# A hybrid decoder layer: where and when the kept gate/up results are loaded

## The chip, the cores and the metric

The kernel runs on one core of one Trainium2 chip. The metric is the device time of one execution in microseconds; the median of 3 runs of the kernel before the change is 1995.07 us (1994.6 to 1999.07).

## The reference, cut to what matters

One decoder layer in fp32: a mixing sub-layer (windowed attention and a convolution group side by side, one output projection) and a dense SwiGLU feed-forward, each between two RMS norms. There are 2048 tokens of width 1024, and the feed-forward's inner width is 2816. The change lies in the feed-forward:

```python
h = rms_norm(x, ffn_pre_g)
h = (silu(h @ w_gate) * (h @ w_up)) @ w_down
x = x + rms_norm(h, ffn_post_g)
```

## The kernel before

**Arithmetic.** Every fp32 operand is split into a rounded high part (ScalarE, line 824) and the rest (a subtraction on VectorE, line 828, which the trace books under line 94, the helper that records all of VectorE's operations). A product is then high·high + high·low + low·high: for a block of 128 output rows, 512 inner and 512 tokens that is 4 × 3 = 12 matmuls (line 85), called a *product* below.

**Tiling.** Tokens go in tiles of 512, and the feed-forward takes two tiles at a time: the first pair (names with @F and @G up to some 1340 us) and the second pair. Each 2 × 2 block product of weights by tokens is done with seven products instead of eight (a Strassen-Winograd scheme): sums of weight blocks (S1 to S4, line 1005, tile `chl`) meet sums of token blocks (T1 to T4). `MATS` lists 22 matrices, gate and up by turns, one for each of 11 blocks of inner rows.

**The stages of a pair.** `stage_pre` (line 916) computes for the first 20 matrices (16 in the second pair) the two products that need only the plain token blocks, and stores their sum to DRAM in `keeps`. `stage_p1` (line 986) then goes through the 22 matrices: five products where a result was kept, seven where not. For a matrix with a kept result:

- `fetch` (lines 1028 to 1032) loads the kept tile into the ring `gb` (two buffers) by SP's queue; it is called in the fourth of the five products of the matrix before (line 1100).
- at the matrix's first product ScalarE copies the kept tile into PSUM bank B (line 1060). This copy is called the *seed*. The first product goes to bank C, the second to bank B, on top of the seed.
- the first product's result y5 is taken out of PSUM by ScalarE into the ring `gb` (line 1071), the second's, x2, into the ring `at` (two buffers, line 1074). VectorE adds later products to them (line 1078), ScalarE applies silu (line 1081), VectorE multiplies gate by up, and the results go to DRAM in `mids` (lines 1088 to 1097).
- weight blocks for the matrix after next are loaded at the last product (lines 1000, 1002).

Beside the first pair's `stage_p1` runs `stage_tsums` (line 1106): for each of the 11 blocks it loads four blocks of w_down (line 1113, ring `wx` of one tile for two of them, ring `fc` of three for the others), waits, makes four subtractions on VectorE (names wx@G and fc@G) and stores each to DRAM (`td`, line 1119). Its `yield` numbers are amounts of work of the main stage: it is pumped at a rate of 0.3.

After `stage_p1` comes `stage_p2` (line 1144), the down projection: its first two token operands use the ring `at` (lines 1162, 1163), the following ones `fa`.

**What sets the order.** Generators are interleaved by their yields, and a tile scheduler turns that into one fixed order of instructions for each engine and each queue. SP's queue issues nearly all transfers, one after the other; an issue that waits for a buffer holds those behind it.

Of the kernel before, what the change touches and what calls it, by code (L numbers as in the profile page):

```python
# [37 lines left out]
def layer_kernel(ctx, tc, x, xT, cols, rows, sinks, relb, onehot, w_in, w_pw, w_out, w_gate, w_up, w_down, out):  # L38
    nc = tc.nc
# [15 lines left out]
    def t_(tag, shape, dt=F32):  # L55
        return sb.tile(list(shape), dt, tag=tag, name=nm(tag), bufs=BUFS[tag])

    def f4(tag, shape=(P, D)):
        return t_(tag, shape)

    def f2(tag, shape=(P, T)):
        return t_(tag, shape)

    def hl(tag):
        return t_(tag, (P, 2, T), F32R)
# [757 lines left out]
    def split_f(x, w):  # L823
        act(w[:, 0], x, AF.Copy)  # L824
        return w

    def lo(x, w, on_pool):
        (ptt if on_pool else vtt)(w[:, 1], x, w[:, 0].bitcast(F32), ALU.subtract)
# [79 lines left out]
    def product(o, w, op, first):  # L908
        n = 0
        for k in range(4):  # L910
            ks = slice(k * P, (k + 1) * P)
            for a, b in ((0, 0), (0, 1), (1, 0)):
                mat(o, w[:, a, ks], op[k][:, b], start=first and n == 0, stop=n == 11, skip_group_check=not first)
                n += 1
# [71 lines left out]
    def stage_p1(ws, ops, mid, keep):  # L986
        PRE = PRES[ws[0]]
        L = f"F{ws[0]}"
        raws = {}
        todo = []  # L990
        for m in range(len(MATS)):
            st = [1, 2, 4, 5, 6] if m < PRE else list(range(7))
            todo += [(m, j, i, len(st)) for j, i in enumerate(st)]

        def loads(m):
            if m < len(MATS):
                lab[0] = L
                src, pr = MATS[m]
                r0 = t_("raw", (P, 2, T))
                nc.sync.dma_start(r0, src[2 * pr].rearrange("p (a b) -> p a b", a=2))  # L1000
                r1 = t_("chl", (P, 2, T))
                nc.sync.dma_start(r1, src[2 * pr + 1].rearrange("p (a b) -> p a b", a=2))
                raws[m] = dict(A11=r0[:, 0], A12=r0[:, 1], A21=r1[:, 0], A22=r1[:, 1])

        def sums(m):
            if m < len(MATS):
                lab[0] = L
                r = raws[m]
                s12 = t_("chl", (P, 2, T))
                r["S1"], r["S2"] = s12[:, 0], s12[:, 1]  # L1010
                vtt(r["S1"], r["A21"], r["A22"], ALU.add)
                vtt(r["S2"], r["S1"], r["A11"], ALU.subtract)
                s34 = t_("chl", (P, 2, T))
                r["S3"], r["S4"] = s34[:, 0], s34[:, 1]
                vtt(r["S3"], r["A11"], r["A21"], ALU.subtract)
                vtt(r["S4"], r["A12"], r["S2"], ALU.subtract)

        wops = {}
        kept = {}

        def split(q):
            if q < len(todo):
                m, j, i, n = todo[q]
                lab[0] = L
                wops[q] = split_f(raws[m][STEPS[i][1]], hl("w"))
                lo(raws[m][STEPS[i][1]], wops[q], ws[0] and i in POOL_LO)

        def fetch(m):
            if m < PRE:
                lab[0] = L  # L1030
                kept[m] = f2("gb")
                nc.sync.dma_start(kept[m], keep[m])

        loads(0)
        sums(0)
        for q in range(AHEAD):
            split(q)
        loads(1)
        fetch(0)
        sg = {}  # L1040
        for q, (m, j, i, nst) in enumerate(todo):
            pre = m < PRE
            gate = MATS[m][0] is w_gate
            pr = MATS[m][1]
            split(q + AHEAD)
            lab[0] = L
            which, an, bn = STEPS[i]
            if len(ops.get(bn, ())) < 4:
                lh.until(f"S{ws[0]}")
                lab[0] = L  # L1050
            if j == 0:
                bk = {}
                if not gate:
                    blocks = {}
                    if pre:
                        blocks[3] = f2("fa")
                        nc.sync.dma_start(blocks[3], mid[0, pr])
                if pre:
                    bk["B"] = mm()
                    act(bk["B"], kept.pop(m), AF.Copy)  # L1060
            first = which not in bk
            if first:
                bk[which] = mm()
            o = bk[which]
            product(o, wops.pop(q), ops[bn], first)
            if i == 0:
                bk["B"] = mm()
                act(bk["B"], o, AF.Copy)
            elif i == 1:
                y5 = f2("gb")  # L1070
                act(y5, o, AF.Copy)
            elif i == 2:
                x2 = f2("at")
                act(x2, o, AF.Copy)  # L1074
            else:
                v = {4: y5, 5: x2}.get(i, o)
                if v is not o:
                    vtt(v, v, o, ALU.add)
                if gate:
                    s = f2("fa")  # L1080
                    act(s, v, AF.Silu)
                    sg[i] = s
                else:
                    s = sg.pop(i)
                    vtt(s, s, v, ALU.mult)
                    blocks[i] = s
                    if i in (3, 4, 6):
                        nc.sync.dma_start(mid[{3: 0, 4: 4, 6: 1}[i], pr], s)
                    if i == 5:
                        a11, a22, a21 = blocks[3], blocks[4], s  # L1090
                        for to, o_, p_, op, q_ in ((5, a22, a21, ALU.add, a22), (3, a21, a11, ALU.subtract, a21),
                                                   (2, a11, a22, ALU.subtract, a11)):
                            (ptt if ws[0] else vtt)(o_, p_, q_, op)
                            nc.sync.dma_start(mid[to, pr], o_)
                    if i == 6:
                        (ptt if ws[0] else vtt)(s, s, blocks[3], ALU.subtract)
                        nc.sync.dma_start(mid[6, pr], s)
            if j == nst - 4:
                sums(m + 1)
            if j == nst - 2:  # L1100
                fetch(m + 1)
            if j == nst - 1:
                loads(m + 2)
            yield 2.76

    def stage_tsums(td):
        L = "G0"
        for pr in range(NF // 2):
            lab[0] = L
            wx = f4("wx", (P, 2, T))  # L1110
            b = [wx[:, 0], wx[:, 1], f2("fc"), f2("fc")]
            for i, (f, n) in enumerate(((0, 0), (0, 1), (1, 0), (1, 1))):
                nc.sync.dma_start(b[i], w_down[2 * pr + f, :, n * T : (n + 1) * T])
            yield 3
            b11, b12, b21, b22 = b
            for to, o, p_, q_ in ((0, b11, b12, b11), (2, b12, b22, b12), (1, b22, b22, b11), (3, b21, b21, b22)):
                lab[0] = L
                vtt(o, p_, q_, ALU.subtract)
                nc.sync.dma_start(td[to, pr], o)
                yield 1  # L1120

    def finish(L, gb, jobs, pool=True):
        lab[0] = L
# [317 lines left out]
    ws, ops = (0, 1), {}  # L1441
# [5 lines left out]
    lh.add("S0", stage_h_sums(ws, ops), lambda: f"P0.{PRE_S0}" in started and "B3" in lb.done)  # L1447
    run(stage_pre(ws, ops, mids[0], keeps[0], Q0))
    lt.add("TS", stage_tsums(td))
    run(stage_p1(ws, ops, mids[0], keeps[0]))  # L1450
    lt.until("TS")
    lc.until("T2")
    lc.rates["T3"] = RC3
    ws, ops = (2, 3), {}
# [9 lines left out]
    run(stage_pre(ws, ops, mids[1], keeps[1]))  # L1464
    lf.until("E0.3")
    run(stage_p1(ws, ops, mids[1], keeps[1]))
    run(stage_p2(ws, mids[1], td, True))

# [62 lines left out]
```

## Time and profile before

| | |
|---|---|
| median of 3 runs | 1995.07 us |
| the profiled execution | 1997.41 us |
| its span, first to last instruction | 1995.4 us |
| mean granted TensorE clock | 0.990 |
| gate/up stage of the first pair | 675 to 987 us |
| down stage of the first pair | 987 to 1340 us |
| gate/up stage of the second pair | 1449 to 1782 us |

A view by windows gives for each stretch the busy time of PE (TensorE's matmuls), PEld (its weight loads), DVE (VectorE), ACT (ScalarE) and POOL (GpSimd), the granted clock and the DMA share. The views of waits list what an engine stood still for: the engine and instruction that waits, an arrow, what released it, and then the us in total, how often, and the longest. A timeline row gives start, duration, engine, line, operation, output<-input, and in square brackets the idle time just before with what ended it. SPq is SP's queue issuing a transfer.

### The profile page before, as it was taken

How to read it: one execution, taken by the hardware profiler on the slowest of the kernel's cores; microseconds unless marked ns; L12 is line 12 of the kernel's file. 1: busy time of each engine (PE TensorE's matmuls, PEld its weight loads, DVE VectorE, ACT ScalarE, POOL GpSimd, SP SyncE). 2: the span in 40 equal slices, each digit the busy share in tenths (PEclk: the TensorE clock that was granted, in tenths of full speed). 3: DMA queues.
4: the chain of work that ended last, by engine and by line, in shares of the span. 5: the costliest groups of instructions: out<-in, count | busy, mean ns of one | idle time of the engine just before them, and what ended most of it. 6: DMA issues, size and time to landing. Idle time of an engine off the chain costs nothing. (4 is left out here: it accounts for less than half of the span.)

```text
span 1995.4 us, 26645 instructions
## 1 busy us (share of the span) xinstructions
PE 1933.4 (97%) x8730; PEld 1547.1 (78%) x8730; DVE 1465.0 (73%) x2578; ACT 952.6 (48%) x1878; POOL 327.0 (16%) x415
## 2 busy tenths in 40 slices
PE   8999999999998999999999999996999999999997
PEld 6877777777777778778878788884788888888886
DVE  4999969995876898887669954576666665555557
ACT  4455354447547533334444555464534433345443
POOL 4011011101122100000000110044423332311003
PEclk9999999999999999999999999998999999999999
DMA  8786657566659868875478876779745542466664
GB/s 302 253 306 216 209 188 256 183 208 219 232 188 347 269 205 268 302 235 173 148 239 266 298 262 201 252 257 334 238 144 177 169 152 92 136 234 191 215 192 146
DMA packets 224811, 444.06 MB, mean 223 GB/s; under 512 B 22137, under 2 KB 47905, under 8 KB 224673
## 3 DMA queue, kind: packets, MB, share of 16 engines
q1 hardware_dynamic: 207584, 420.35, 63.7%
q10 hardware_dynamic: 17088, 22.02, 3.0%
q8 instruction: 68, 1.11, 0.2%
q14 instruction: 71, 0.57, 0.1%
HBM read 327.46 MB, written 114.83 MB: 222 GB/s over the span
## 5 line engine op out<-in xcount | busy, mean ns | idle before, releaser
L94 DVE SCALAR_TENSOR_TENSOR fc@C<-glu@C,colt,fc@C 128x512 f32<-128x512 f32 x480 | 356.5, 756 | 2.8
L85 PE MATMUL mm@F<-hl@H,w@F 128*128 128x512 f32 x1056 | 253.4, 390 | 5.6 <-ACT mm@F L953 4.6
L85 PEld LDWEIGHTS mm@F<-hl@H,w@F 128*128 128x128 f32 x1056 | 197.5, 188 | 48.5 <-ACT mm@F L953 6.3
L85 PE MATMUL mm@G<-hl@G,hl@G 128*128 128x512 f32 x924 | 227.7, 392 | 2.9 <-DVE hl@G L94 1.8
L85 PE MATMUL mm@A<-hl@A,w@A 128*128 128x512 f32 x840 | 209.5, 397 | 4.7 <-ACT w@A L127 2.3
L85 PEld LDWEIGHTS mm@G<-hl@G,hl@G 128*128 128x128 f32 x924 | 171.7, 188 | 39.6 <-DVE hl@G L94 2.5
L824 ACT ACTIVATE w@F<-chl@F 128x512 fp32r<-128x512 f32 x220 | 135.2, 625 | 136.4 <-PE mm@F L85 130.7
L85 PE MATMUL mm@G<-w@G,hl@G 128*128 128x512 f32 x876 | 199.4, 389 | 0.0
L85 PEld LDWEIGHTS mm@G<-w@G,hl@G 128*128 128x128 f32 x876 | 164.4, 188 | 34.1
L85 PEld LDWEIGHTS mm@A<-hl@A,w@A 128*128 128x128 f32 x840 | 156.6, 189 | 43.5 <-issue 3.1
L94 DVE TENSOR_TENSOR w@F<-chl@F,w@F 128x512 fp32r<-128x512 f32 x198 | 145.5, 739 | 37.5 <-ACT w@F L824 37.2
L85 PE MATMUL mm@F<-mid@H,w@F 128*128 128x512 f32 x528 | 138.8, 411 | 15.6 <-ACT mm@F L953 10.4
L85 PE MATMUL mm@F<-ql@H,w@F 128*128 128x512 f32 x528 | 130.7, 395 | 13.9 <-ACT mm@F L1060 5.3
L85 PEld LDWEIGHTS mm@F<-mid@H,w@F 128*128 128x128 f32 x528 | 104.6, 199 | 40.6 <-ACT mm@F L953 11.5
L85 PE MATMUL mm@F<-p@H,w@F 128*128 128x512 f32 x528 | 129.0, 389 | 0.0
L85 PEld LDWEIGHTS mm@F<-ql@H,w@F 128*128 128x128 f32 x528 | 99.7, 190 | 37.8 <-ACT mm@F L1060 6.5
L85 PE MATMUL mm@F<-x@H,w@F 128*128 128x512 f32 x528 | 126.8, 391 | 0.0
L85 PEld LDWEIGHTS mm@F<-p@H,w@F 128*128 128x128 f32 x528 | 99.0, 188 | 20.7 <-ACT at@F L1074 0.2
L85 PEld LDWEIGHTS mm@F<-x@H,w@F 128*128 128x128 f32 x528 | 98.4, 188 | 21.5 <-DVE fc@C L94 0.8
L495 POOL TENSOR_SCALAR_AFFINE_SELECT p@B<-p@B 128x512 f32<-128x512 f32 x62 | 52.3, 853 | 363.4 <-ACT p@B L493 362.0
L127 ACT ACTIVATE w@A<-raw@A 128x512 fp32r<-128x512 f32 x110 | 67.4, 625 | 93.0 <-PE mm@A L85 61.0
L94 DVE TENSOR_TENSOR w@G<-raw@G,w@G 128x512 fp32r<-128x512 f32 x73 | 52.2, 715 | 68.6 <-ACT w@G L824 67.7
(302 smaller groups left out, 3299.7 us busy)
## 6 DMA issues: line engine op xcount, KB each, us to landing
mids<-fa@F SPq DMA_DIRECT2D x154, 256.0 KB, 2.6
raw@A<-w_in SPq DMA_DIRECT2D x55, 512.0 KB, 4.5
w@A<-lo_in SPq DMA_DIRECT2D x84, 256.0 KB, 3.4
fc@G<-mids SPq DMA_DIRECT2D x77, 256.0 KB, 3.5
fa@G<-mids SPq DMA_DIRECT2D x75, 256.0 KB, 4.4
gb@F<-keeps SPq DMA_DIRECT2D x72, 256.0 KB, 4.1
w@W<-fold SPq DMA_DIRECT2D x32, 512.0 KB, 5.3
chl@F<-w_gate SPq DMA_DIRECT2D x22, 512.0 KB, 4.0
```

Source lines behind the costliest of these rows:

```text
L85: r = nc.tensor.matmul(*args, **kw)
L94: r = op(*args, **kw)
L127: act(w[:, 0], raw, AF.Copy)
L495: nc.gpsimd.affine_select(out=pg[:, kb].rearrange("p (i q) -> p i q", q=P), in_=pg[:, 1].rearrange("p (i q) -> p i q", q=P), compare_op=AL ...
L824: act(w[:, 0], x, AF.Copy)
```

## The change

There are four edits. The first pair's kept results are loaded by GpSimd's queue, the second pair's still by SP's. y5 goes to the ring `at` beside x2, so that the ring `gb` holds kept results alone within the stage. `fetch(m + 1)` is called in the second product of a matrix (j = 1). In `stage_tsums` 5 units instead of 3 lie between a block's loads and its first subtraction, and 0.5 instead of 1 after each subtraction: 7 in all as before.

```diff
@@ stage_p1, fetch
-                nc.sync.dma_start(kept[m], keep[m])
+                (nc.sync if ws[0] else nc.gpsimd).dma_start(kept[m], keep[m])
@@ stage_p1, first product of a matrix
-                y5 = f2("gb")
+                y5 = f2("at")
@@ stage_p1
-            if j == nst - 2:
+            if j == 1:
                 fetch(m + 1)
@@ stage_tsums
-            yield 3
+            yield 5
...
-                yield 1
+                yield 0.5
```

What SP's queue does around one kept load in the middle of the first pair's gate/up stage: weight loads and stores of the w_down sums (td) around it. Before:

```order
L1119 DMA td<-fc@G_1373_8310 128x512
L1113 DMA wx@G_1403_8516<-w_down 128x512 x2
L1119 DMA td<-fc@G_1372_8309 128x512
L1113 DMA fc@G_1404_8517<-w_down 128x512
L1088 DMA mids_4716<-fa@F_1310_7903 128x512
L1032 DMA gb@F_1351_8163<-keeps_4719 128x512
L1113 DMA fc@G_1405_8518<-w_down 128x512
L1119 DMA td<-wx@G_1403_8516 128x512
```

And the same place of SP's queue after the change:

```order
L1119 DMA td<-wx@G_1371_8308 128x512
L1119 DMA td<-fc@G_1373_8310 128x512
L1119 DMA td<-fc@G_1372_8309 128x512
L1113 DMA wx@G_1403_8516<-w_down 128x512 x2
L1088 DMA mids_4716<-fa@F_1311_7903 128x512
L1113 DMA fc@G_1404_8517<-w_down 128x512
L1113 DMA fc@G_1405_8518<-w_down 128x512
L1119 DMA td<-wx@G_1403_8516 128x512
```

The kept load (L1032) stands behind two stores and a store to mids before, and is gone from SP's queue after; the loads of the w_down blocks still follow the stores of the block before. On GpSimd the 20 loads stand in one piece with nothing between them, and each waits only for the seed that frees its buffer.

The second place is ScalarE at that seed, with the evictions of y5 (L1071) and x2 (L1074) and the high parts of weights (L824). Before:

```order
L1071 ACTIVATE gb@F_1339_8092<-mm@F_1338_8079 128x512
L824 ACTIVATE w@F_1340_8096<-chl@F_1320_7952 128x512
L824 ACTIVATE w@F_1347_8126<-chl@F_1342_8113 128x512
L1074 ACTIVATE at@F_1341_8111<-mm@F_1337_8077 128x512
L824 ACTIVATE w@F_1349_8145<-chl@F_1342_8113 128x512
L824 ACTIVATE w@F_1352_8165<-chl@F_1343_8116 128x512
L1060 ACTIVATE mm@F_1358_8192<-gb@F_1351_8163 128x512
L824 ACTIVATE w@F_1356_8187<-chl@F_1343_8116 128x512
```

After:

```order
L824 ACTIVATE w@F_1336_8072<-chl@F_1329_7997 128x512
L1060 ACTIVATE mm@F_1358_8192<-gb@F_1344_8119 128x512
L824 ACTIVATE w@F_1340_8096<-chl@F_1320_7952 128x512
L1071 ACTIVATE at@F_1339_8090<-mm@F_1338_8077 128x512
L824 ACTIVATE w@F_1348_8128<-chl@F_1342_8113 128x512
L1074 ACTIVATE at@F_1341_8111<-mm@F_1337_8075 128x512
```

The seed of the next matrix (mm@F_1358) has moved from behind the evictions of y5 and x2 to ahead of them.

The third place is VectorE where a block of w_down sums meets the addition to y5 (gb@F before, at@F_1252 after). Before:

```order
L94 TENSOR_TENSOR chl@F_1272_7645<-chl@F_1272_7645,raw@F_1264_7599 128x512
L94 TENSOR_TENSOR chl@F_1273_7648<-raw@F_1264_7599,chl@F_1272_7645 128x512
L94 TENSOR_TENSOR wx@G_1257_7529<-fc@G_1259_7531,wx@G_1257_7529 128x512
L94 TENSOR_TENSOR gb@F_1252_7503<-gb@F_1252_7503,mm@F_1250_7488 128x512
L94 TENSOR_TENSOR fc@G_1259_7531<-fc@G_1259_7531,wx@G_1257_7529 128x512
L94 TENSOR_TENSOR at@F_1254_7521<-at@F_1254_7521,mm@F_1251_7490 128x512
```

After:

```order
L94 TENSOR_TENSOR w@F_1263_7580<-chl@F_1256_7526,w@F_1263_7580 128x512
L94 TENSOR_TENSOR chl@F_1273_7644<-raw@F_1264_7599,chl@F_1272_7641 128x512
L94 TENSOR_TENSOR wx@G_1258_7531<-fc@G_1260_7533,wx@G_1258_7531 128x512
L94 TENSOR_TENSOR fc@G_1260_7533<-fc@G_1260_7533,wx@G_1258_7531 128x512
L94 TENSOR_TENSOR at@F_1252_7501<-at@F_1252_7501,mm@F_1250_7486 128x512
L94 TENSOR_TENSOR fc@G_1259_7532<-fc@G_1259_7532,fc@G_1260_7533 128x512
L94 TENSOR_TENSOR at@F_1254_7521<-at@F_1254_7521,mm@F_1251_7488 128x512
```

The sum that reads a w_down block (wx@G<-fc@G) stands ahead of y5's addition in both, with one more sum between them after the change.

At the end of the stage, TensorE's order has 36 matmuls of the second pair's out-projection (names tr@W) ahead of the first matmul of the down stage (mm@G), which before stood between the down stage's first ones.

## The prediction

> **What bounds the kernel now.** I read the page's busy line first, then the table by stage, then what TensorE waits for inside the one stage that the change touches most.
>
> ```profile
> PE 1933.4 (97%) x8730; PEld 1547.1 (78%) x8730; DVE 1465.0 (73%) x2578; ACT 952.6 (48%) x1878; POOL 327.0 (16%) x415
> 675.00:987.00 312.00, 299.16 (x1304) 244.38 (x1303) 261.67 (x419) 116.82 (x209) 0.00 (x0) 0.99 0.68 224
> 1449.00:1782.00 333.00, 333.00 (x1469) 275.40 (x1469) 200.13 (x261) 129.15 (x229) 97.14 (x68) 1.00 0.46 154
> ```
>
> TensorE is busy for 1933.4 of 1995.4 us, and the change neither adds nor removes a matmul. So it can only give back TensorE's idle time, or add some. The second and third lines are the gate/up stages of the first and the second pair (columns: window, its us, then busy us of PE, PEld, DVE, ACT, POOL, then the granted clock, DMA share, GB/s). The first pair has 312.00 − 299.16 = 12.8 us of idle PE; the second has none (333.00 of 333.00), so its sixteen kept loads, moved as well, can gain nothing. GpSimd computes nothing in the first pair (0.00).
>
> Next, the waits of PE from 675 to 987 us (us in total, times, longest), and under them the largest wait of ScalarE there:
>
> ```profile
> PE mm@F L85 <- ACT mm@F L1060: 5.3, 2, 4.2
> PE mm@F L85 <- ACT w@F L824: 3.0, 1, 3.0
> PE mm@F L85 <- DVE gb@F L94: 2.7, 3, 1.1
> PE mm@F L85 <- ACT gb@F L1071: 1.0, 1, 1.0
> PE mm@F L85 <- DVE fa@F L94: 0.9, 1, 0.9
> PE mm@F L85 <- ACT mm@F L953: 0.3, 1, 0.3
> ACT mm@F L1060 <- DMA gb@F<-keeps: 56.1, 16, 10.1
> ```
>
> The six PE rows add to 13.2, which is the idle time. L1060 is the seed: ScalarE copies the kept result into PSUM, and the matrix's product on bank B may start only then. ScalarE itself waits 56.1 us for the kept tiles, up to 10.1 at once. Most of that costs nothing; it costs where PE runs dry behind it.
>
> **The change, part by part.** *1. The kept loads come sooner.* The issue and landing of a kept load now:
>
> ```profile
> L1032 SPq DMA_DIRECT2D gb@F<-keeps x36: 319/402/698, 668.8 to 1633.1; - x36
> DMA to landing us min/median/max: 2.6/3.8/7.0
> 797.71 0.42 SPq L1032 DMA_DIRECT2D gb@F<-keeps  x1
> 803.07 0.60 ACT L1060 ACTIVATE mm@F<-gb@F 128x512 f32<-128x512 f32 x1 [10.05 <-DMA gb@F<-keeps]
> 803.61 0.61 ACT L824 ACTIVATE w@F<-chl@F 128x512 fp32r<-128x512 f32 x1
> 804.27 0.74 PE L85 MATMUL mm@F<-ql@H,w@F 128*128 128x512 f32 x2 [2.98 <-ACT w@F L824]
> 861.69 0.43 SPq L1032 DMA_DIRECT2D gb@F<-keeps  x1
> 866.44 0.60 ACT L1060 ACTIVATE mm@F<-gb@F 128x512 f32<-128x512 f32 x1 [8.31 <-DMA gb@F<-keeps]
> 867.09 1.07 PE L85 MATMUL mm@F<-ql@H,w@F 128*128 128x512 f32 x2 [4.19 <-ACT mm@F L1060]
> 867.96 2.76 PE L85 MATMUL mm@F<-mid@H,w@F 128*128 128x512 f32 x6
> 870.52 1.64 PE L85 MATMUL mm@F<-mb@H,w@F 128*128 128x512 f32 x6
> 872.00 2.44 PE L85 MATMUL mm@F<-ql@H,w@F 128*128 128x512 f32 x10
> 874.28 1.52 PE L85 MATMUL mm@F<-yt@H,w@F 128*128 128x512 f32 x6
> 875.64 1.52 PE L85 MATMUL mm@F<-mid@H,w@F 128*128 128x512 f32 x6
> ```
>
> At both places SP issues the load about 5 us before the seed, with a transfer of 3.8, so whatever delays SP lands on the seed. At 804 the 3.0 that the wait table books on L824 belongs here too: that split is queued behind a seed that held ScalarE for 10.05 us. At 867 PE waits 4.2 and is then slow: 24 matmuls from 867.09 to 874.28 take 7.19 us, where six at pace take 875.64 − 874.28 = 1.36, so 24 take 5.44. That is 1.75 more, which goes with the wait.
>
> The order shows the loads alone on GpSimd's queue, held only by the seed that frees their buffer (two matrices back). A matrix is five products of 2 × 1.36 = 2.72, so 13.6 us, and the lead becomes up to 27 us against 5. I take the two rows, 5.3 + 3.0, as gone, and 1.75 with them: **−10.05**. The 1.1 at 704, the smaller of the two L1060 waits, is not banked:
>
> ```profile
> 704.47 1.43 PE L85 MATMUL mm@F<-ql@H,w@F 128*128 128x512 f32 x5 [1.14 <-ACT mm@F L1060]
> 711.34 1.66 PE L85 MATMUL mm@F<-yt@H,w@F 128*128 128x512 f32 x6 [1.13 <-DVE gb@F L94]
> 700.00:760.00 60.00, 56.77 (x248) 46.04 (x247) 57.11 (x93) 23.52 (x42) 0.00 (x0) 1.00 0.64 211
> 795.00:825.00 30.00, 27.02 (x118) 21.99 (x119) 27.44 (x46) 10.50 (x19) 0.00 (x0) 1.00 0.85 288
> 825.00:860.00 35.00, 34.44 (x151) 27.77 (x150) 27.43 (x45) 12.37 (x22) 0.00 (x0) 1.00 0.88 295
> 860.00:890.00 30.00, 25.81 (x107) 20.84 (x106) 26.01 (x43) 9.22 (x17) 0.00 (x0) 0.94 0.70 226
> ```
>
> DVE is busy 57.11 of 60 us from 700 to 760, and PE waits for it 7 us later anyway: there what is late next is DVE, and I give the 1.1 back: **+1.1**. The large two lie where DVE has room: from 795 to 890 it idles 2.6 + 7.6 + 4.0 = 14.1 us, and the gain asks 8.95 of them.
>
> *2. The issue on GpSimd.* SP is spared 20 issues of 0.40. What writing one such load costs on GpSimd is in no row: this kernel has no load there yet. What GpSimd and DVE cost each other is shown only for computing, in the second pair:
>
> ```profile
> L94 DVE TENSOR_TENSOR w@F<-chl@F,w@F 128x512 fp32r<-128x512 f32 x106 | 72.0, 684 | 4.9 <-ACT w@F L824 4.8
> L94 DVE TENSOR_TENSOR w@F<-chl@F,w@F 128x512 fp32r<-128x512 f32 x83 | 67.4, 815 | 29.6 <-ACT w@F L824 29.3
> L1093 POOL TENSOR_TENSOR fa@F<-fa@F,fa@F x31: 1287/1298/1628, 1472.5 to 1780.9; 128x512 f32<-128x512 f32 x31
> L1060 ACT ACTIVATE mm@F<-gb@F x36: 590/602/604, 675.9 to 1636.9; 128x512 f32<-128x512 f32 x36
> ```
>
> The first row is DVE's split in the first pair, the second the same work beside GpSimd's 68 operations: 684 becomes 815 ns. Over its 200.13 us DVE loses at most about 200.13 × 131/815 = 32 us, 0.47 per GpSimd operation. Ends for the 20 loads: nothing, and 20 × 0.47 = 9.4 us of DVE, of which the stage can hide what DVE idles. The seeds start at 675.9 and come every 13.6 us, so seven fall before 760, where DVE idles least: 7 × 0.47 = 3.3. I take half of that, **+1.6**, nearer to nothing since a load computes nothing on GpSimd; the ends stay 0 and 9.4.
>
> *3. Longer lead for the w_down sums, and y5 in the x2 ring.*
>
> ```profile
> 793.51 0.69 DVE L94 TENSOR_TENSOR wx@G<-fc@G,wx@G 128x512 f32<-128x512 f32 x1 [1.30 <-DMA fc@G<-w_down]
> 794.12 0.68 DVE L94 TENSOR_TENSOR gb@F<-gb@F,mm@F 128x512 f32<-128x512 f32 x1
> 794.85 1.66 PE L85 MATMUL mm@F<-yt@H,w@F 128*128 128x512 f32 x6 [1.01 <-DVE gb@F L94]
> ```
>
> A sum that waits for its w_down block holds y5's addition behind it, and PE waits 1.0: this is the form of the 2.7 on DVE. The order moves the sums by one to four DVE operations only, at this place the waiting sum still stands ahead of y5's addition, and the w_down loads still follow the stores that free their ring. Gain between −1.0 (a new such wait) and 2.7; I take **−0.7**, near the one place where an operation of 0.69 is put in between.
>
> *4. Hand-over to the down stage.* In the first pair y5 now shares a ring with the down stage's first two operands:
>
> ```profile
> 995.07 0.38 SPq L1163 DMA_DIRECT2D at@G<-mids  x1
> 1008.78 0.68 DVE L94 TENSOR_TENSOR fa@F<-fa@F,gb@F 128x512 f32<-128x512 f32 x1
> 1018.48 2.79 PE L85 MATMUL mm@G<-hl@G,hl@G 128*128 128x512 f32 x11 [1.09 <-ACT hl@G L824]
> ```
>
> The operand load of 995.07 must now wait for y5's last reader (1008.78, about 1004 once no down matmul stands ahead of it). The order puts 36 matmuls of the out-projection (8.2 us at 1.36 per six) ahead of the first down matmul, more than load and split need (3.8 + two of 0.7). Ends: −1.1 (the wait of 1018) and +3; I take **+0.5**.
>
> **Sum.** −10.05 + 1.1 + 1.6 − 0.7 + 0.5 = −7.55. The profiled execution took 1997.41 (span 1995.4), so it would take 1989.9; it lies 2.34 over the median of 1995.07, and against the median the forecast is **1987.5**.
>
> **The rivals.** *A. DVE becomes the bound.* For it: 57.11 of 60 busy from 700, and 27.44 of 30 around the wait at 804. If the 3.0 there comes back as a wait for DVE, and GpSimd costs the 3.3 in full, the sum is −10.05 + 1.1 + 3.0 + 3.3 − 0.7 + 0.5 = −2.85: 1992.2. Against it: the 7.6 us that DVE idles right behind.
>
> *B. Slower: GpSimd gets to write its loads only when DVE pauses.* Place: 675 to 760, seven seeds, DVE at 57.11 of 60. A load delayed past its 27 us of lead costs landing plus seed, 3.8 + 0.6 = 4.4 us of PE. Four late seeds are 17.6; against the −7.55 the time is 1995.07 + 10.05 = 2005. It decides from two late seeds on (8.8 > 7.55). Against it: GpSimd's computing in the second pair ran at a median of 1298 ns with a shortest of 1287 and a longest of 1628, so DVE held it for 0.34 us at most. The Trainium skill, "SBUF — State Buffer", section "Who interferes with whom", has this mechanism as a trap: a load issued from GpSimd stands still while DVE is in a two-port mode, and elsewhere on that page 620 ns become about 3100. The same section says that tensor_tensor has no such mode and bars only GpSimd's reads; by the trap each load would land 2.5 us later, which is an estimate from that page and far inside the lead, so by it the sum stays. No run yet shows a load issued there.
>
> *C. It doesn't do what it says.* With five products a matrix the fetch moves from the fourth to the second, two products, and the w_down sums hardly move. If landing is slow because the DMA engines are full (share 0.85 and 0.88 from 795 to 860), the waits stay: 1995. Against it: 10.05 us of waiting for a transfer of 3.8, with the issue itself late.
>
> **How the numbers follow.** A measurement of this kernel tells about 0.3% from no change, 6 us: faster is below 1989.1, slower above 2001. The forecast has 0.60 (1981 to 1991, over its bounds: the low end is 1995.07 less 12.8 idle and 1.75 clock), A 0.18, C 0.07, B 0.15. Of the forecast's 0.60 some five sixths lie below 1989.1: faster 0.50; same is the rest of it with A, C and the mild end of B, 0.37; slower 0.13. The range runs from 1981 to 2000: B's upper part and the odd end are left out.
>
> **What would show it.** Right: the wait of L1060 for keeps near 0 in the first pair, the issues of L1032 there on GpSimd with 15 us or more to the seed; PE idle from 675 to 987 down from 12.8 to about 4; no slow matmuls at 867; DVE's split still near 684 ns. A: new PE waits for DVE (at@F or w@F) between 795 and 890, or that split above 700 ns. B: landing times on GpSimd's queue above 20 us and L1060 still waiting before 760. Wrong at the hand-over: PE idle over 3 us before the first down matmuls. The whole is wrong if the stage shortens by 9 us and the span doesn't.

## The result and the profile after

The changed kernel is slower: 2006.1 us median against 1998.59 before (10 runs each, the three shown above among them), ratio 1.0041 with a 95% interval of 1.0031 to 1.0050. On another chip, run again beside the rest, it was 1.0031 (1.0020 to 1.0041). The forecast was a gain of 0.4%. Part of the distance between 2006.1 and the forecast 1987.5 is the basis: it was reckoned from a median of 1995.07 over three runs, and over ten runs the kernel before stands at 1998.59. What is left is a gain of 7.55 us forecast and a loss of 7.5 measured. Executions of one kernel scatter by some 5 us to either side here, so a single profile settles nothing under that size; the ratios do.

The profile of after, its busy line and the stretches that the prediction used for before (the first pair's gate/up stage, and the hand-over behind it):

```profile
PE 1941.8 (97%) x8730; PEld 1551.4 (77%) x8730; DVE 1470.4 (73%) x2578; ACT 955.1 (48%) x1878; POOL 337.2 (17%) x435
675.00:987.00 312.00, 297.48 (x1272) 241.26 (x1271) 256.79 (x412) 114.14 (x202) 9.68 (x18) 0.98 0.68 225
990.00:1020.00 30.00, 30.00 (x134) 24.83 (x133) 15.99 (x27) 13.81 (x27) 0.00 (x0) 1.00 0.58 188
```

The same 312 us hold 1272 matmuls where they held 1304. At full pace (1.36 us per six) 32 matmuls are 7.3 us; the spans differ by 2002.2 − 1995.4 = 6.8. So the loss lies in this stage. PE idles 14.5 us instead of 12.8, which is 1.7 of it; the other 5.6 is busy time, since a matmul takes longer on average, with the granted clock at 0.98 instead of 0.99. That split is this pair's alone: two further profiles, only_lead with the order of before and the changed kernel again (both below), hold 1312 and 1276 matmuls in the same 312 us, with 10.2 and 15.5 us of idle PE at the same granted clock of 0.99. So the stage's loss of 7 to 8 us stands, and its split into idle and slower time doesn't. The hand-over has no idle PE at all.

What PE waits for there, and below it ScalarE's waits that concern the seed:

```profile
PE mm@F L85 <- DVE at@F L94: 8.4, 4, 3.8
PE mm@F L85 <- DVE fa@F L94: 4.9, 5, 2.2
PE mm@F L85 <- DVE w@F L94: 0.5, 1, 0.5
PE mm@F L85 <- ACT at@F L1071: 0.4, 1, 0.4
PE mm@F L85 <- ACT mm@F L1060: 0.3, 1, 0.3
...
ACT mm@F L1060 <- DVE at@F L94: 36.3, 11, 7.9
```

The 5.3 and 3.0 us behind kept loads are gone, as forecast. In their place stand 8.4 and 4.9 us behind VectorE: the additions to y5 and x2, and the multiplications that read a product out of its bank. The seed too now waits for VectorE: it stands so early in ScalarE's line that its bank is still being read.

The loads on GpSimd's queue, and VectorE's split beside them:

```profile
L1032 POOL DMA_DIRECT2D gb@F<-keeps x20: 538/538/753, 669.1 to 918.2; - x20
POOL gb@F L1032 <- ACT mm@F L1060: 221.8, 17, 21.5
L94 DVE TENSOR_TENSOR w@F<-chl@F,w@F 128x512 fp32r<-128x512 f32 x105 | 71.2, 685 | 4.4 <-ACT w@F L824 4.4
```

GpSimd writes a load in 538 ns and is early: it waits for the seed that frees the buffer, up to 21.5 us. VectorE's split takes 685 ns against 684. The second wait of the stage, on VectorE and TensorE:

```profile
704.47 0.69 DVE L94 TENSOR_TENSOR wx@G<-fc@G,wx@G 128x512 f32<-128x512 f32 x1 [2.11 <-DMA fc@G<-w_down]
707.16 0.69 DVE L94 TENSOR_TENSOR chl@F<-chl@F 128x512 f32<-128x512 f32 x1 [1.33 <-DMA chl@F<-w_up]
710.24 0.68 DVE L94 TENSOR_TENSOR at@F<-at@F,mm@F 128x512 f32<-128x512 f32 x1
713.30 0.68 DVE L94 TENSOR_TENSOR at@F<-at@F,mm@F 128x512 f32<-128x512 f32 x1
714.04 2.93 PE L85 MATMUL mm@F<-yt@H,w@F 128*128 128x512 f32 x6 [3.78 <-DVE at@F L94]
716.76 2.76 PE L85 MATMUL mm@F<-mid@H,w@F 128*128 128x512 f32 x6
719.32 3.05 PE L85 MATMUL mm@F<-hl@H,w@F 128*128 128x512 f32 x11
...
815.98 2.93 PE L85 MATMUL mm@F<-yt@H,w@F 128*128 128x512 f32 x6 [2.50 <-DVE at@F L94]
...
839.35 2.79 PE L85 MATMUL mm@F<-mid@H,w@F 128*128 128x512 f32 x6 [2.16 <-DVE fa@F L94]
```

VectorE stands 2.11 us for a w_down block and 1.33 for a weight block, with the additions in line behind both. The last product of the matrix (yt) may go on top of bank B only when y5's addition has read it, so PE waits 3.78. Then it is slow: twelve matmuls from 714.04 to 719.32 take 5.28 us instead of 2.72. Two more such places follow, after waits of 2.50 and 2.16.

### The profile page after: what moved, and what is told of

Its sections match the earlier page's. It is cut to its first block, busy times and chain, and to the rows that moved or that the text cites. A ratio compares the mean times of both kernels' runs of the same rounds, so it can differ in the third digit from the quotient of the medians.

```text
span 2002.2 us, 26678 instructions
## 1 busy us (share of the span) xinstructions
PE 1941.8 (97%) x8730; PEld 1551.4 (77%) x8730; DVE 1470.4 (73%) x2578; ACT 955.1 (48%) x1878; POOL 337.2 (17%) x435
## 5 line engine op out<-in xcount | busy, mean ns | idle before, releaser
L824 ACT ACTIVATE w@F<-chl@F 128x512 fp32r<-128x512 f32 x220 | 136.0, 625 | 181.3 <-PE mm@F L85 176.3
L85 PEld LDWEIGHTS mm@F<-p@H,w@F 128*128 128x128 f32 x528 | 99.3, 188 | 20.7
```

The costliest lines, as they stand in the source:

```text
L85: r = nc.tensor.matmul(*args, **kw)
```

## The experiments

The experiments test three theories: 1, the order that follows from y5's move is to blame; 2, GpSimd as issuer is; 3, VectorE bounds this stage and the gain can't be had. The last two columns show the stage in one profile of each kernel: idle PE from 675 to 890 us, while the w_down sums run (215 us less the busy time), and the matmuls in that window. Two profiles of one order differ by up to 2.6 us and 8 matmuls there (before and only_lead).

| kernel | ratio to before (95%) | idle PE, us | matmuls |
|---|---|---|---|
| before | 1 | 12.8 | 874 |
| changed | 1.0041 (1.0031 to 1.0050) | 13.4 | 850 |
| only_lead | 0.9994 (0.9980 to 1.0008) | 10.2 | 882 |
| only_queue | 1.0013 (0.9999 to 1.0027) | 11.9 | 870 |
| only_ring | 0.9996 (0.9985 to 1.0008) | 10.5 | 879 |
| seed_tied | 1.0007 (0.9994 to 1.0020) | 13.8 | 861 |
| nosub_before | 0.9986 (0.9978 to 0.9995) | 6.1 | 906 |
| nosub_after | 1.0004 (0.9994 to 1.0013) | 7.4 | 907 |
| ring_pool_sums | 1.0106 (1.0093 to 1.0119) | 28.4 | 769 |
| ring_act_queue | 1.0010 (1.0001 to 1.0020) | 15.5 | 860 |
| before_sums_tied | 0.9931 (0.9916 to 0.9947) | 2.0 | 935 |
| ring_sums_tied | 0.9970 (0.9960 to 0.9981) | 5.8 | 913 |
| after_sums_tied | 1.0033 (1.0019 to 1.0047) | 11.6 | 867 |
| ring_seed_tied | 1.0001 (0.9987 to 1.0016) | 14.1 | 861 |
| order_after_on_sp | 1.0037 (1.0022 to 1.0052) | 15.6 | 836 |
| order_ring_on_gpsimd | 1.0016 (1.0005 to 1.0028) | 12.3 | 865 |
| order_tied_on_gpsimd | 0.9950 (0.9934 to 0.9967) | 4.1 | 922 |
| changed, again | 1.0031 (1.0020 to 1.0041) | 14.6 | 852 |
| order_after_sp_only | 1.0092 (1.0072 to 1.0112) | 19.6 | 807 |
| order_after_engines_only | 1.0089 (1.0069 to 1.0108) | 15.6 | 858 |

In the tied kernels (names with sums_tied or order_tied) the sums run on to between 916 and 937 us. Over the whole stage, 675 to 987 us, before_sums_tied still idles 2.0 us, ring_sums_tied 7.9 and after_sums_tied 14.2; order_after_engines_only idles 21.8.

### The parts one by one

only_queue, the first edit alone:

```diff
-                nc.sync.dma_start(kept[m], keep[m])
+                (nc.sync if ws[0] else nc.gpsimd).dma_start(kept[m], keep[m])
```

> Before with one edit only: the first pair's kept loads go by GpSimd's queue (y5 stays in the ring gb, fetch in the fourth product, w_down pacing 3 and 1). Theory 1 (the order is to blame: y5's move out of the ring gb lets the scheduler set the seeds so early on ScalarE that they wait there for a PSUM bank, and draws the next matrix's products forward): without that move the queue alone gives the gain that was forecast, ratio to before 0.994 to 0.998, the seeds' waits for keeps near 0. Theory 2 (the loads on GpSimd cost VectorE or land late): slower than before, ratio 1.002 to 1.005, nearly the whole loss. Theory 3 (VectorE is the bound of this stage whatever is done): 0.999 to 1.001, the waits for kept loads replaced by waits for VectorE.

only_ring, the second alone:

```diff
-                y5 = f2("gb")
+                y5 = f2("at")
```

> Before with one edit only: y5 goes to the ring at, the kept loads stay on SP's queue in the fourth product. Theory 1: slower, ratio 1.003 to 1.006, with seeds that wait on ScalarE for VectorE (over 30 us in the first pair) and waits of TensorE for at@F. Theory 2: 0.997 to 1.000. Theory 3: 0.999 to 1.001.

only_lead, the two others (j == 1; yields 5 and 0.5):

> Before with the two other edits only: fetch in the second product and the w_down pacing 5 and 0.5. Each engine's and queue's order of instructions is that of before but for tile numbers, so all theories say ratio 0.999 to 1.001; this is the measure of what no change looks like.

Measured: none of the three differs from before beyond its interval. For only_lead that was certain, since the scheduler writes the same order with and without it, and it does so beside queue and ring as well: **two of the four edits do nothing.** The loss shows only where queue and ring stand together. Theory 1 missed on only_ring (it had it slower, though the waits that it named came) and on only_queue (it had it faster). Theory 2 had only_ring and missed on only_queue, whose 1.0013 lies below the expected 1.002 to 1.005. Theory 3 had only_ring; for only_queue it said 0.999 to 1.001 with VectorE in place of the kept loads, and there PE waits 7.7 us for splits on ScalarE and 4.1 for VectorE. In only_ring the kept loads are on time from SP's queue as well:

```profile
PE mm@F L85 <- DVE at@F L94: 6.6, 4, 3.4
PE mm@F L85 <- DVE fa@F L94: 3.4, 4, 1.8
PE mm@F L85 <- DVE w@F L94: 0.5, 1, 0.5
ACT mm@F L1060 <- DVE at@F L94: 36.4, 10, 8.5
ACT mm@F L1060 <- DVE fa@F L94: 2.3, 1, 2.3
ACT mm@F L1060 <- DMA gb@F<-keeps: 1.0, 2, 0.5
```

The seeds' wait for keeps falls from 56.1 to 1.0 us, and the time stays: PE now waits for VectorE. In only_queue the loads stay late, although GpSimd's queue holds nothing else:

```profile
POOL gb@F L1032 <- ACT fa@F L1081: 129.9, 9, 19.2
POOL gb@F L1032 <- DVE fa@F L94: 123.2, 9, 17.7
...
ACT mm@F L1060 <- DMA gb@F<-keeps: 50.6, 16, 7.1
```

The releasers are the readers of y5: in a ring shared with y5, a kept result gets the buffer of a y5 still in use. So the ring made the loads early, not the queue and not the earlier call.

seed_tied, the changed kernel with the seeds held back in ScalarE's order:

```diff
-                    act(bk["B"], kept.pop(m), AF.Copy)
+                    seed = act(bk["B"], kept.pop(m), AF.Copy)
+                    # first pair: seed placed behind the last x2 taken out
+                    tc.add_manual_dep(seed.ins, behind[0].name, ...)
```

> The changed kernel with a dependency that sets each seed of the first pair behind the taking out of the x2 of the matrix before, on ScalarE's order alone. Theory 1: the seeds no longer wait for a bank, the order of products comes back, and the loss goes: ratio to before 0.994 to 0.999. Theory 2: 1.003 to 1.005 as the changed kernel. Theory 3: 0.999 to 1.002.

It takes most of the loss back (1.0007) and gains nothing; no single theory had that, though theory 3's range holds it.

### Is VectorE the bound?

nosub_before and nosub_after leave out the subtraction of `stage_tsums`; loads and stores stay.

```diff
-                vtt(o, p_, q_, ALU.subtract)
```

> Before without the 44 subtractions of the w_down sums: the blocks are loaded and stored as they are, so the down stage works on wrong sums; transfers are the same, VectorE has 30 us less to do from 675 to 890 us. If VectorE with its waits in line is what bounds that stretch (theory 3), the 2.7 of waits for y5 and most of the clock's loss go, and what stays are the waits for kept loads: ratio 0.994 to 0.998. If the kept loads alone bind (the prediction), 0.998 to 1.000.

> The changed kernel without the same 44 subtractions (same wrong sums). Theory 3: with VectorE relieved the early kept loads show their gain at last, so TensorE's idle time in the first pair's gate/up stage falls below 6 us, ratio to before 0.990 to 0.994 and below the other kernel of this pair. If the loads on GpSimd are harmful by themselves, it stays above the other kernel by about 8 us.

Up to 890 us both relieve the stage: 6.1 and 7.4 us of idle PE instead of 13, and 906 and 907 matmuls instead of 874 and 850. So the sums on VectorE have a part in what holds TensorE up there. The ratios are not theory 3's, which had 0.994 to 0.998 and 0.990 to 0.994. The 0.9986 of nosub_before lies in the range for kept loads that bind alone, and nosub_after, which was to be the faster of the two, is 0.18% above it. Leaving instructions out also gave other orders elsewhere, so these two say something of the stage only, and whether VectorE is its bound they leave open.

ring_pool_sums, only_ring with the subtractions on GpSimd (`ptt` for `vtt`):

> Before with y5 in the ring at (kept loads on SP) and the 44 subtractions of the w_down sums on GpSimd, which is idle there. Theory 3: VectorE loses 30 us of work and 11 us of standing for w_down blocks, and gets back at most 44 x 0.47 = 21 us as stretching beside GpSimd; the idle TensorE falls from 13 to some 3 us: ratio 0.991 to 0.996. If VectorE is not the bound: 0.999 to 1.002.

A clear miss, 1.06% slower:

```profile
L1118 POOL TENSOR_TENSOR fc@G<-fc@G,fc@G 128x512 f32<-128x512 f32 x11 | 17.5, 1594 | 0.9
L94 DVE TENSOR_TENSOR w@F<-chl@F,w@F 128x512 fp32r<-128x512 f32 x66 | 55.7, 848 | 0.7 <-ACT w@F L824 0.6
...
PE mm@F L85 <- DVE fa@F L94: 18.1, 5, 7.6
PE mm@F L85 <- DVE at@F L94: 9.8, 1, 9.8
```

A subtraction that took VectorE 0.69 us takes GpSimd 1.42 to 1.59 on average, and VectorE's own split goes from 684 to 848 ns beside it. VectorE also stands 40.0 us for weight blocks in the stage, against 16.8 in only_ring. Which of these makes the loss was not separated.

ring_act_queue, only_ring with the kept loads on ScalarE's queue (`nc.scalar`):

> As only_ring (y5 in the ring at), but the first pair's kept loads are issued from ScalarE's queue instead of SP's. It tells whether the 8 us between only_ring and the changed kernel come from GpSimd as issuer or from taking the loads out of SP's line. GpSimd as the cause: 0.998 to 1.001 as only_ring. SP's line and the order that follows: 1.002 to 1.005 as the changed kernel.

Its 1.0010 is the upper edge of the first range, and its interval reaches the lower edge of the second, so it decides nothing.

### Where the sums stand

In before SP's queue looks like this ahead of the late kept load of 797.71:

```profile
794.23 0.33 SPq L1119 DMA_DIRECT2D td<-wx@G  x1
795.43 0.33 SPq L1119 DMA_DIRECT2D td<-fc@G  x1
796.51 0.68 DVE L94 TENSOR_TENSOR fa@F<-fa@F,gb@F 128x512 f32<-128x512 f32 x1
797.23 0.42 SPq L1088 DMA_DIRECT2D mids<-fa@F  x1
```

The first two are stores of w_down sums, and the first is issued right when the sum that had waited for its block (793.51 + 0.69) is done. The store to mids just ahead of the kept load is issued when VectorE's multiplication with y5 is done (796.51 + 0.68). A sum that stands still on VectorE so holds y5's addition and multiplication behind it and, by their stores, the kept load on SP's queue. At the costlier place, ahead of the kept load of 861.69, it is a weight block that VectorE stands for, not a sum:

```profile
859.39 0.69 DVE L94 TENSOR_TENSOR chl@F<-chl@F 128x512 f32<-128x512 f32 x1 [2.40 <-DMA chl@F<-w_gate]
860.61 0.69 DVE L94 TENSOR_TENSOR fa@F<-fa@F,gb@F 128x512 f32<-128x512 f32 x1
861.32 0.33 SPq L1088 DMA_DIRECT2D mids<-fa@F  x1
```

Of the next four kernels three set every subtraction behind the last addition to y5 or x2 that the program wrote before it, by a tie on VectorE's order alone (`added` holds that addition); the fourth, ring_seed_tied, keeps seed_tied's order and changes the issuer.

```diff
-                vtt(o, p_, q_, ALU.subtract)
+                d = vtt(o, p_, q_, ALU.subtract)
+                tc.add_manual_dep(d.ins, added[0].name, ...)
```

> The changed kernel with each subtraction of the w_down sums set behind the last addition to y5 or x2 that was written before it, on VectorE's order alone. If the changed kernel is slower because its order puts waiting sums ahead of those additions, the loss goes: ratio to before 0.995 to 0.999, waits of TensorE for at@F under 3 us. If GpSimd as issuer costs the 8 us: 1.003 to 1.005.

> only_ring with the same tie (kept loads on SP's queue). Sums in the way as the cause of the waits that took the place of the kept loads': 0.993 to 0.998. If any order of VectorE costs the same, since it is the engine that bounds: 0.998 to 1.001. Beside after_sums_tied it gives the price of GpSimd as issuer in another order: 0 if harmless, 0.3 to 0.4% if it is the cause.

> Before with the same tie and nothing else. If the sums in front of y5's addition were worth only their 2.7 us of waits: 0.998 to 1.000. If spreading the sums frees more (the stretch to 890 us is crowded, behind it VectorE has room): 0.994 to 0.998.

> seed_tied with the kept loads on SP's queue instead of GpSimd's. Third pair for the issuer: GpSimd harmless says the same as seed_tied, 0.999 to 1.002; GpSimd as the cause of the 8 us says 0.996 to 0.998. For the ring: held seeds say no better than only_ring, 0.999 to 1.001, if VectorE bounds.

**before_sums_tied is the fastest kernel of the study**, 1984.82 us median, 0.69% (0.53 to 0.84) under before, with none of the four edits:

```profile
675.00:987.00 312.00, 310.01 (x1364) 254.70 (x1363) 266.74 (x429) 123.78 (x222) 0.00 (x0) 1.00 0.71 235
PE mm@F L86 <- DVE fa@F L95: 0.9, 1, 0.9
PE mm@F L86 <- ACT gb@F L1072: 0.7, 1, 0.7
PE mm@F L86 <- ACT w@F L825: 0.4, 1, 0.4
ACT mm@F L1061 <- DMA gb@F<-keeps: 59.8, 19, 6.2
```

(One added line shifts the line numbers by one.) The seeds wait for kept loads as before, 59.8 us, 19 times; but the longest wait is 6.2 instead of 10.1, and PE never waits behind one. It idles 2.0 us and gets 60 matmuls more done, better than either expectation. The kept loads come as late on the whole, and that costs nothing. The sums' own waits on VectorE for w_down blocks fall from 11.3 to 1.1 us in the stage. SP's queue, though, stands for the stores of the sums no less than in before (its two lines first, then those of before_sums_tied):

```profile
SPq L1119 <- DVE wx@G L94: 20.9, 14, 3.8
SPq L1119 <- DVE fc@G L94: 11.2, 15, 2.1
SPq L1127 <- DVE wx@G L95: 19.5, 16, 3.5
SPq L1127 <- DVE fc@G L95: 17.8, 16, 2.7
```

So the tie relieved VectorE's line; that it also took stores out of the kept loads' way does not show in these sums. The scheduler writes the orders of all engines anew around the tie; which of the moved rows make the gain is not shown.

With the ring edit the same tie gives only 0.9970, on the same chip: **moving y5, with the order that follows from it, costs 0.4% once the sums are out of the way.** On the changed kernel it gives nothing (1.0033): the range that was to speak for GpSimd as the cause. But the issuer and the order differ there both, and the next kernels part them.

### Order or issuer

In the next three the order of all instructions in the stage but the kept loads is held on each engine by a chain of dependencies of the kind above, copied from another kernel; only who issues the kept loads differs. The fourth is the changed kernel again, on the same chip.

> The changed kernel with the kept loads of the first pair on SP's queue, and with the changed kernel's own order of all other instructions of that stage held by dependencies on each engine. If the order is what costs: 1.002 to 1.005 as the changed kernel. If GpSimd as issuer costs: 0.998 to 1.001 as only_ring.

> The changed kernel (kept loads on GpSimd's queue) with the order of only_ring on the four engines and queues held in that stage. Order as the cause: 0.998 to 1.001. Issuer as the cause: 1.003 to 1.005.

> before_sums_tied, the fastest so far, in its own order held, with the kept loads on GpSimd's queue in place of SP's and nothing else. GpSimd harmless: 0.991 to 0.995 as before_sums_tied. GpSimd costing 0.3 to 0.4%: 0.996 to 0.999.

> The changed kernel itself, once more on this chip: 1.003 to 1.005 by every theory. It is the other end for the first two.

**The order costs, with or without GpSimd:** the changed kernel's order on SP's queue gives 1.0037, the changed kernel 1.0031 beside it. From order_after_on_sp, the two waits that matter:

```profile
PE mm@F L47 <- DVE at@F L47: 9.1, 5, 3.8
PE mm@F L47 <- DVE fa@F L47: 5.0, 5, 2.4
```

(All its instructions are issued through a wrapper, line 47.) They are the changed kernel's 8.4 and 4.9 again. The profiles show one more thing that goes with this order, VectorE's waits for weight blocks from 675 to 900 us (the first two lines are of before, the others of the changed kernel):

```profile
DVE chl@F L94 <- DMA chl@F<-w_gate: 6.1, 5, 2.4
DVE chl@F L94 <- DMA chl@F<-w_up: 5.7, 4, 3.3
DVE chl@F L94 <- DMA chl@F<-w_gate: 13.7, 7, 2.9
DVE chl@F L94 <- DMA chl@F<-w_up: 7.0, 5, 1.9
```

That is 11.8 us before and 20.7 after, 19.4 in the changed kernel again and 20.3 in order_after_on_sp, against 13.3 in only_ring. That this is the loss is not shown: order_ring_on_gpsimd has 19.4 at 1.0016.

Four pairs give the price of the issuer at one order, GpSimd less SP: −0.06% here, +0.06% (seed_tied), +0.20% (only_ring) and +0.19% (before_sums_tied). Each pair's intervals overlap, and three of the pairs were measured on different chips, so the points lie between nothing and 0.2%, 4 us. A small price is not ruled out: order_ring_on_gpsimd lies between its two expectations, and above before by more than its interval, where only_ring does not.

The last two try to place it within the order: SP's order alone from the changed kernel, or that of the three engines alone, the rest from only_ring.

> only_ring, its own order held on TensorE, VectorE and ScalarE, with the changed kernel's order on SP's queue alone. If SP's order (weight loads behind other issues, so VectorE stands longer for them) makes the loss: 1.003 to 1.005. If the engines' order makes it: 0.998 to 1.001.

> only_ring, its own order held on SP's queue, with the changed kernel's order on TensorE, VectorE and ScalarE. Engines' order as the cause: 1.003 to 1.005. SP's order as the cause: 0.998 to 1.001. About 1.002 in both: each makes half.

Both miss: each half costs 0.9%, twice the whole. Both mixtures are worse than either complete order. That this is because SP's queue then issues in another sequence than the engines work is my reading, not shown. Which rows of the changed order cost the 0.4% stays open.

## Why the prediction was wrong, point by point

- **The bound.** That TensorE's idle time in the first pair's gate/up stage is what can be won or lost was right, and so was the second pair at nothing.
- **The 10.05 us (5.3 + 3.0 + 1.75): the step that failed.** "I take the two rows ... as gone" was true of the rows and false of the time. The waits for kept loads went (0.3 us left), and 13.8 us of waits for VectorE came. Three of the signs that I had named for being right did appear: seeds no longer held by loads, 20 us and more of lead from the third load on, and the split at 685 ns. I compared VectorE's idle time (14.1 us from 795 to 890) with the gain, as if any of it could be used. But 12.0 us of that idle time were themselves waiting for weight and w_down blocks, with the additions in line behind. Room on an engine that waits in order is no slack. only_ring shows it without GpSimd: seeds on time, ratio 0.9996. The loss on top is the order's: order_after_on_sp has it, 1.0037, with the loads on SP.
- **The cause of the late loads.** I put it on SP's lateness and let an earlier load cure it. Both late loads stood behind a store that waited for VectorE, and before_sums_tied shows what relieves it: with the sums moved on VectorE and the loads as late on the whole, PE stops waiting.
- **The clock, 1.75.** The term was right in kind and went the other way: waits of 3.78, 2.50 and 2.16 us are each followed by slow matmuls. Busy time in the stage grew by 5.6 us for its matmuls, in this profile.
- **The 1.1 given back at 704.** Right: the very place where PE would meet VectorE, with 3.78 instead of 1.13.
- **GpSimd, +1.6 (0 to 9.4).** Within its ends: 685 against 684 ns on VectorE, 0 to 4 us by the points of the pairs.
- **w_down, −0.7.** These edits do nothing; only_lead has before's order. The moved operations that I read in the order came from the other two edits. The rival that the change doesn't do what it says had this half.
- **The hand-over, +0.5.** It was −1.1, the wait of 1018 gone: PE waits for nothing from 985 to 1060.
- **The rivals.** B had the sign and the size (2005) by luck, through a mechanism that didn't occur: no load was late on GpSimd (all kept loads landed within 6.9 us of their issue). The Trainium skill's "SBUF — State Buffer", section "Who interferes with whom", has it that a probe with tensor_tensor did not show the stall that tensor_copy showed; the trace agrees, with 538 ns at the median and 753 at most for writing a load. A had the mechanism, VectorE in place of the kept loads, but I gave it 3.0 us, and with GpSimd's 3.3 that still left a gain of 2.85. What it lacked was that a wait moved to VectorE comes with a new order, which can be worse than the old one.
- **A reading.** The six rows of PE's waits add to 13.2 and not to the idle time, which is 12.8 by the window's row.

## What to carry to other kernels

A wait that ends with a transfer names what came last, not what was slow: follow the transfer's issue back through its queue to what that queue stood behind, here stores that waited for VectorE. Before idle time of an in-order engine is counted as room, look at what it waits for and who is in line behind. And where a scheduler writes the order, a buffer's move is a new order of everything around it: build each edit alone, compare orders first (two of four edits changed none), and hold one order while a queue or a buffer is tested.

## What the runs showed of the hardware

TensorE ran slow after waits of 2.16, 2.50 and 3.78 us, six matmuls in 2.6 to 2.7 us instead of 1.36, with a granted clock of 0.57 from 839 to 843, 0.62 from 816 to 820 and 0.57 from 714 to 721 us. A wait of 2.98 us in before had left it at full speed, with 1.00 from 804 to 808 us. The length of the wait alone does not decide it in these traces.
